# A hybrid attention and convolution block on one core: x loaded a second time in transposed form, and the small vectors as columns

## The chip, the core and the metric

The kernel runs as one program on one core of one Trainium2 chip. The metric is the device time of one execution in microseconds. Before the change it is 1059.32 us, the median of three runs (1058.66 to 1060.2).

Four engines compute: TensorE (PE in the profile, with its weight loads as PEld), VectorE (DVE), ScalarE (ACT) and GpSimd (POOL). SyncE (SP) issues most of the transfers from the chip's memory. Each engine takes its instructions in the order in which the program emits them.

## The reference

One layer over 256 tokens of width 2048, in float32, cut to its course:

```python
xn = rms_norm(x, norm1_g)                      # x: (256, 2048)
q, k, v, ga, gg = split(xn @ w_in)             # 1024 columns each
att = diff_attention(rope(rms_norm(q)), rope(rms_norm(k)), v, lam)
u = ga * sigmoid(gg)
u = silu(layer_norm(causal_depthwise_conv(u, conv_w, conv_b)))   # 31 taps
h = x + concatenate([rms_norm(att), u]) @ w_out
hn = rms_norm(h, norm2_g)
out = h + (silu(hn @ w_gate) * (hn @ w_up)) @ w_down             # hidden 5632
```

## The kernel before

**Products.** A float32 product is made of three matmuls in a shorter format: each operand is split into a rounded part (`hi`) and the rest (`lo`), and hi x hi, lo x hi and hi x lo are summed in PSUM. The tokens are two tiles of 128 rows (m = 0, 1); the weights stream in from memory once.

**Chunks.** All weight work is a list of chunks, mostly of 512 KB. For each chunk the SP queue loads `raw` (line 330), ACT rounds it to `whi` (334), DVE takes the rest `wlo` (343), and PE multiplies: a first half with `whi` (373 and 374) and a second half with `wlo` (379). `raw` has four buffers (tag raw), and every third chunk from chunk 7 on takes one of the two larger `wb` buffers instead (1237). `whi` and `wlo` have four buffers each, so rounding chunk n waits until PE has done chunk n - 4. Up to chunk 4 the rounding is emitted one chunk ahead of the multiplication, from chunk 5 on two chunks ahead (line 476).

The blocks at the start, in the order of the list: the five blocks for the convolution's columns, of which block 0 (chunks 0 to 4, width 256) and block 1 (chunks 5 to 8, width 256) come first; block 2 begins with chunk 9 (width 512). Each block accumulates in two PSUM tiles of the pool `acc`, which has four. Block 2 therefore takes the two tiles that block 0 had.

**Side work.** Everything beside the weight chunks is written as Python generators. Each chunk's `multiply` calls `resume()` twice, after its first half and after its second half (391 and 396), and each call carries every generator to its next `yield`. So a `yield` puts off an emission by half a chunk; the order within each engine's queue is fixed by it. These matter here:

- `x_part` and `x_rest` (498 to 521): x arrives by rows, in five column parts (`XPARTS`, line 54: tiles k = 0-1, 2-3, 4-7, 8-11, 12-15 of 128 columns), into `h`, which also keeps x for the residual. PE transposes each 128 x 128 piece (502), ACT makes `lhi` times the norm's gain (240) and DVE makes `llo` (241). In between, ACT sums the squares of x (491), four column groups of 512 for both m; DVE adds the four sums (518), POOL makes the root `rstd1` (217 and 218), and `normed` is set.
- `glu_done` (535 to 564), one per convolution block: it waits for `normed`, then ACT makes `sig` from the block's sums (544), two resumes later DVE makes `u` from them (549), which is the last use of the block's two PSUM tiles; three resumes later PE transposes `u` (557), and then the 30 taps per channel tile are queued for DVE (569), to be given out by credit: 1.30 a resume, less what other DVE work is charged.
- `gain_columns` (153): the 58 rows of gains and biases are loaded as rows by the ACT queue (148), transposed on PE (155) and copied to `cols` (156).
- `late_constants` (177): the convolution's weights as two tiles of 31 rows (172), the q and k gains and lambda vectors (174), the rotary tables (175), all loaded on the SP queue ahead of chunk 5's weights; PE transposes the convolution's weights in eight pieces (182) and ACT copies them to `cw` (183).
- `warm_up` (140): 14 transposes of the identity at the start, and 5 more after the first part of x.

**The load order on SP** is set by `before` (1252 to 1255): part i of x, two transfers each, stands just ahead of chunk i's weights for i = 0 to 4, and the late constants ahead of chunk 5's.

Of the kernel before, what the change touches and what calls it, by code (L numbers as in the profile page):

```python
# [13 lines left out]
F32 = mybir.dt.float32  # L14
# [5 lines left out]
P = 128  # L20
D = 2048
S = 256
NM = S // P
# [4 lines left out]
CC = 1024  # L28
NCT = CC // P
W = 31  # L30
FF = 5632
KD = D // P
N = 512
# [15 lines left out]

NK = 2  # L50

WARM = (14, 5)

XPARTS = (range(0, 2), range(2, 4), range(4, 8), range(8, 12), range(12, 16))

# [17 lines left out]
HK = KD // 2  # L73
# [35 lines left out]
def tile_block(  # L109
    ctx: ExitStack,  # L110
    tc: tile.TileContext,
    x, conv_w, gains, vecs, rope, wts, out, placed_at,
):
    nc = tc.nc
    PSUM = bass.MemoryType.PSUM
    act, dve, pool, pe, sp = nc.scalar, nc.vector, nc.gpsimd, nc.tensor, nc.sync
# [16 lines left out]
    ident = const.tile([P, P], F32, tag="ident", name="ident")  # L133
# [6 lines left out]
    def warm_up(n):  # L140
        warm = aux_ps.tile([P, N], F32, tag="aux", name="ps_warm")
        for _ in range(n):
            pe.transpose(warm[:, :P], ident, ident)

    warm_up(WARM[0])

    rows = pre.tile([NR, P], F32, tag="rows", name="rows", bufs=1)
    act.dma_start(out=rows, in_=gains)

    act.copy(small.tile([P, 8], F32, tag="rsq", name="first"), neghalf)  # L150
    cols = once.tile([P, NR], F32, tag="cols", name="cols")

    def gain_columns():
        ps = aux_ps.tile([P, N], F32, tag="aux", name="ps_cols")
        pe.transpose(ps[:, :NR], rows, ident[:NR, :NR])
        act.copy(cols, ps[:, :NR])

    def col(key, k):
        return cols[:, AT[key] + k : AT[key] + k + 1]

    cw = pre.tile([P, LINE * 2], F32, tag="cw", name="cw", bufs=1)[:, : NCT * W].rearrange("p (c w) -> p c w", c=NCT)
    gcs = {}
    neg_lam = once.tile([P, 1], F32, tag="neg_lam", name="neg_lam")
    cw_rows = [pre.tile([W, N], F32, tag="va", name="cw_rows") for _ in range(CC // N)]
    rt = pre.tile([P, NM, 2, DH], F32, tag="vb", name="rt")
    gb = pre.tile([P, 2, DH], F32, tag="att", name="gb", bufs=4)
    lamv = pre.tile([P, 4, DH], F32, tag="vc", name="lamv")

    def late_loads():
        flat = conv_w.rearrange("o w i c -> (o w i) c")  # L170
        for i in range(CC // N):
            sp.dma_start(out=cw_rows[i], in_=flat[:, i * N : (i + 1) * N])
        for t, v in ((gb, vecs[:2]), (lamv, vecs[2:])):
            sp.dma_start(out=t, in_=v.rearrange("(o v) d -> o v d", o=1).to_broadcast(list(t.shape)))
        sp.dma_start(out=rt, in_=rope.rearrange("(m p) c d -> p m c d", p=P))

    def late_constants():
        late_loads()
        yield from lag(4)
        pw = aux_ps.tile([P, N], F32, tag="aux", name="ps_cw")  # L180
        for ct in range(NCT):
            pe.transpose(pw[:, ct * W : (ct + 1) * W], cw_rows[ct * P // N][:, ct * P % N : ct * P % N + P], ident[:W, :W])
        act.copy(cw.rearrange("p c w -> p (c w)"), pw[:, : NCT * W])
        while not normed:
            yield
        yield from lag(16)
        act.mul(cols[:, AT["sg"] : AT["sg"] + 2], cols[:, AT["sg"] : AT["sg"] + 2], 1.0 - LAMBDA_INIT)

        act.mul(gb[:, 0, :], gb[:, 0, :], 1.0 / math.sqrt(DH))
        hd = DH // 2  # L190
        for i, key in enumerate("qk"):
            for m in range(NM):
                t = pre.tile([P, 2, DH], F32, tag=f"gcs{key}{m}", name=f"gcs{key}{m}", bufs=1)
                pool.tensor_tensor(t[:, 0, :], rt[:, m, 0, :], gb[:, i, :], ALU.mult)
# [18 lines left out]
    def rsqrt_mean(dst, ss, n, eps):  # L213

        k = dst.shape[-1]
        t = small.tile([P, 8], F32, tag="rsq", name="rsq")
        pool.tensor_scalar(t[:, :k], ss, 1.0 / n, eps, ALU.mult, ALU.add)
        pool.tensor_tensor(dst, t[:, :k], neghalf[:, :k], ALU.pow)
# [5 lines left out]
    def lhs_pair(pfx, k):  # L224
        if k % 2 == 0:
            halves[pfx] = lhs_two(pfx, k)
        return tuple(t[:, k % 2, :] for t in halves[pfx])
# [9 lines left out]
    def split_scaled(pair, src, scale):  # L237

        hi, lo = pair
        act.activation(hi, src, AF.Copy, scale=scale)  # L240
        dve.scalar_tensor_tensor(lo, src, scale, hi.bitcast(F32), ALU.mult, ALU.subtract)  # L241
# [6 lines left out]
    def start(gen):  # L248
        running.append(gen)
# [6 lines left out]
    def lag(n):  # L256
        for _ in range(n):
            yield
# [33 lines left out]
    before = {}  # L292
# [192 lines left out]
    xT = {}  # L485
    rstd1 = [once.tile([P, 1], F32, tag=f"rstd1_{m}", name=f"rstd1_{m}") for m in range(NM)]
    ss1 = [small.tile([P, D // N], F32, tag=f"ss1_{m}", name=f"ss1_{m}", bufs=1) for m in range(NM)]

    def square_sum(src, accum, **kw):
        junk = pre.tile([P, N], F32, tag="junk", name="junk", bufs=1)  # L490
        act.activation(junk[:, : src.shape[-1]], src, AF.Square, accum_out=accum, **kw)

    def x_load(ks):
        cs = slice(ks[0] * P, (ks[-1] + 1) * P)
        for m in range(NM):
            sp.dma_start(out=h[m][:, cs], in_=x[m * P : (m + 1) * P, cs])

    def x_part(ks):
        for k in ks:
            ps = aux_ps.tile([P, N], F32, tag="aux", name="ps_x")  # L500
            for m in range(NM):
                pe.transpose(ps[:, m * P : (m + 1) * P], h[m][:, k * P : (k + 1) * P], ident)
            xT[k] = lhs_pair("x", k)
            split_scaled(xT[k], ps[:, :S], col("g1", k))

    def x_rest():
        c = 0
        for part in XPARTS[1:]:
            x_part(part)
            yield  # L510
            yield
            if part[-1] % (N // P) == N // P - 1:
                for m in range(NM):
                    square_sum(h[m][:, c * N : (c + 1) * N], ss1[m][:, c : c + 1])
                c += 1
        for m in range(NM):
            ss = small.tile([P, 1], F32, tag="ss1", name="ss1")
            dve.tensor_reduce(ss, ss1[m], AX.X, ALU.add)
            rsqrt_mean(rstd1[m], ss, D, EPS)
        yield  # L520
        normed.append(True)
# [728 lines left out]
        j0 += nb  # L1250

    for c, part in enumerate(XPARTS):
        before[c] = lambda part=part: x_load(part)
    before[0] = lambda: (x_load(XPARTS[0]), gain_columns(), x_part(XPARTS[0]), warm_up(WARM[1]), start(x_rest()))
    before[len(XPARTS)] = lambda: start(late_constants())
    run_chunks()


_FLAT = {"x": (S, D), "conv_w": (1, W, 1, CC)}
_WEIGHTS = {"w_in": (D, 5120), "w_out": (D, D), "w_gate": (D, FF), "w_up": (D, FF), "w_down": (FF, D)}  # L1260


# [28 lines left out]
```

## Time and profile before

| what | value |
|---|---|
| median of three runs | 1059.32 us (1058.66 to 1060.2) |
| the profiled execution's own time | 1059.67 us |
| its span in the profile | 1057.9 us |
| mean granted TensorE clock | 0.998 |
| busy share of PE, DVE, ACT, POOL | 98%, 84%, 63%, 13% |
| moved by DMA | 248.10 MB |

The span is the time from the first to the last instruction in the trace; 1.77 us of the profiled execution lie outside it. A timeline row gives the start, the time taken, the engine, the source line, the operation, the written and read tiles, the count of merged instructions, and in brackets the idle time before it with what ended it. A row of the table by stretches gives, for each engine, the busy time and the number of instructions, then the granted clock, the share in which the DMA engines were busy, and the rate.

### The profile page before, as it was taken

Reading aid. Unit: us, or ns where it says so; the run is one execution under the profiler, and the core shown is the slowest. Engines: PE = TensorE matmul, PEld = TensorE weight load, DVE = VectorE, ACT = ScalarE, POOL = GpSimd, SP = SyncE. Lnnn points to the kernel's source line nnn. Section 1 sums busy time; section 2 is a strip of 40 time slices with the busy share of each in tenths; the row PEclk is TensorE's granted clock in tenths of the full one; section 3 lists DMA queues with packets and bytes.
Section 4 is the critical chain, followed back from the end, with each engine's and each line's share of the span. In section 5 each row is a group of like instructions: output and inputs, shape, how many; then the busy total and the mean of one; then the engine's idle time right before and its main releaser. Section 6 shows DMA issues by size and latency. Waiting matters only on the chain.

```text
span 1057.9 us, 13283 instructions
## 1 busy us (share of the span) xinstructions
PE 1038.6 (98%) x4780; PEld 859.5 (81%) x4780; DVE 883.5 (84%) x1103; ACT 667.0 (63%) x852; POOL 136.5 (13%) x182
## 2 busy tenths in 40 slices
PE   8999999999999999999999999999999999999998
PEld 7988888878888887787888888888888888888776
DVE  4799989889666489989979679899896698989984
ACT  6544556757666556676676565776865566668661
POOL 0030023211100100010001120000101111001021
PEclk9999999999999999999999999999999999999999
DMA  8655555454546668997969998979978999879985
GB/s 297 211 176 191 192 178 183 145 171 148 171 140 228 211 209 256 289 265 223 321 198 292 277 308 266 276 225 312 264 228 256 292 289 334 241 223 283 285 216 111
DMA packets 63166, 248.10 MB, mean 235 GB/s; under 512 B 7044, under 2 KB 8510, under 8 KB 55676
## 3 DMA queue, kind: packets, MB, share of 16 engines
q1 hardware_dynamic: 48432, 199.51, 53.3%
q0 software_dynamic: 14608, 47.72, 23.4%
q8 instruction: 37, 0.61, 0.2%
q14 instruction: 29, 0.24, 0.1%
q10 hardware_dynamic: 60, 0.03, 0.0%
HBM read 238.84 MB, written 8.39 MB: 234 GB/s over the span
## 4 chain that ended last, share of the span: by engine, by line
PE 56%; DVE 7%; issue 2%; ACT 1%; POOL 0%; DVEq 0%; ACTq 0%; POOLq 0%
PE q L1074 10%; PE q L1075 10%; PE q L1079 10%; PE q L1053 8%; PE q L1054 8%; PE q L1055 8%; DVE wl L1036 1%; DVE wlo L343 1%; DVE wl L1035 1%; DVE wt L1024 1%; PE ps_a L891 1%; PE acc L379 1%; PE acc L374 1%; PE acc L373 1%; DVE wt L1025 0%
## 5 line engine op out<-in xcount | busy, mean ns | idle before, releaser
L334 ACT CAST whi<-raw 128x1024 fp32r<-128x1024 f32 (+1 forms) x261 | 268.9, 1046 | 116.1 <-PE q L1075 48.5
L343 DVE TENSOR_TENSOR wlo<-raw,whi 128x1024 fp32r<-128x1024 f32 (+1 forms) x188 | 228.0, 1220 | 84.8 <-ACT whi L334 84.6
L373 PE MATMUL acc<-whi,lhi 128*128 128x512 f32 (+1 forms) x448 | 168.6, 381 | 3.4 <-ACT lhi L240 2.7
L374 PE MATMUL acc<-whi,llo 128*128 128x512 f32 (+1 forms) x448 | 167.0, 377 | 0.5 <-DVE llo L241 0.4
L1031 ACT CAST wh<-wt 128x2048 fp32r<-128x2048 f32 x58 | 110.8, 1910 | 38.2 <-DVE wt L1026 37.9
L1036 DVE TENSOR_TENSOR wl<-wt,wh 128x2048 fp32r<-128x2048 f32 x58 | 132.8, 2289 | 2.0 <-ACT wh L1031 1.2
L338 POOL DMA_DIRECT2D wlo<-in_wts_dram x73 | 63.9, 875 | 522.1 <-ACT wlo L337 487.6
L1035 DVE TENSOR_TENSOR wl<-wb,wh 128x1536 fp32r<-128x1536 f32 x58 | 101.7, 1754 | 29.7 <-ACT wh L1030 29.7
L1074 PE MATMUL q<-whi,chi 128*128 128x512 f32 x320 | 125.3, 392 | 0.0
L1075 PE MATMUL q<-whi,clo 128*128 128x512 f32 x320 | 124.6, 389 | 0.0
L379 PE MATMUL acc<-wlo,lhi 128*128 128x512 f32 (+1 forms) x448 | 114.3, 379 | 1.4 <-DVE wlo L343 1.4
L1053 PE MATMUL q<-wh,fhi 128*128 128x512 f32 x280 | 109.8, 392 | 3.1 <-DVE sum L1155 1.4
L1055 PE MATMUL q<-wl,fhi 128*128 128x512 f32 x280 | 109.0, 389 | 0.0
L1054 PE MATMUL q<-wh,flo 128*128 128x512 f32 x280 | 109.0, 389 | 0.0
L569 DVE SCALAR_TENSOR_TENSOR y<-upad,cw,y 128x256 f32<-128x256 f32 x240 | 104.1, 488 | 4.4 <-ACT y L562 3.9
L373 PEld LDWEIGHTS acc<-whi,lhi 128*128 128x128 f32 x448 | 85.3, 190 | 18.9 <-ACT lhi L240 3.1
L374 PEld LDWEIGHTS acc<-whi,llo 128*128 128x128 f32 x448 | 85.5, 191 | 15.7 <-DVE llo L241 0.9
L1030 ACT CAST wh<-wb 128x1536 fp32r<-128x1536 f32 x58 | 85.4, 1473 | 17.5 <-issue 10.9
L379 PEld LDWEIGHTS acc<-wlo,lhi 128*128 128x128 f32 x448 | 79.6, 188 | 16.6 <-DVE wlo L343 2.3
L1079 PE MATMUL q<-wlo,chi 128*128 128x512 f32 x320 | 86.3, 391 | 0.0
L337 ACT ACTIVATE wlo<-raw 128x1024 fp32r<-128x1024 f32 x73 | 77.1, 1056 | 0.0
L1024 DVE TENSOR_TENSOR wt<-wb 128x1024 f32<-128x1024 f32 x58 | 70.8, 1222 | 0.5
(216 smaller groups left out, 1689.1 us busy)
## 6 DMA issues: line engine op xcount, KB each, us to landing
raw<-in_wts_dram SPq DMA_DIRECT2D x259, 512.0 KB, 5.4
wb<-in_wts_dram SPq DMA_DIRECT2D x57, 1024.0 KB, 7.4
wlo<-in_wts_dram POOLq DMA_DIRECT2D x73, 512.0 KB, 8.9
out_dram<-sum POOLq DMA_DIRECT2D x22, 256.0 KB, 6.4
out_dram<-h POOLq DMA_DIRECT2D x8, 256.0 KB, 5.7
h<-in_x_dram SPq DMA_DIRECT2D x6, 256.0 KB, 7.5
wb<-in_wts_dram POOLq DMA_DIRECT2D x1, 1024.0 KB, 8.3
h<-in_x_dram SPq DMA_DIRECT2D x4, 128.0 KB, 3.3
```

Source lines behind the costliest of these rows:

```text
L334: act.copy(c["hi"], c["raw"])
L343: dve.tensor_tensor(c["lo"], c["raw"], c["hi"].bitcast(F32), ALU.subtract)
L373: pe.matmul(ps[m], xhi[:, ms], hi[:, j, :], start=c["first"] and j == 0, stop=False)
L374: pe.matmul(ps[m], xlo[:, ms], hi[:, j, :], start=False, stop=False)
L379: pe.matmul(ps[m], xhi[:, ms], lo[:, j, :], start=False, stop=c["last"] and j == nk - 1)
L1036: dve.tensor_tensor(c["lo"][:, :4], c["t"], c["hi"][:, :4].bitcast(F32), ALU.subtract)
L1053: pe.matmul(ps, fhi[:, f, p, :], c["hi"][:, w], start=bool(first), stop=False)
L1054: pe.matmul(ps, flo[:, f, p, :], c["hi"][:, w], start=False, stop=False)
L1055: pe.matmul(ps, fhi[:, f, p, :], c["lo"][:, w], start=False, stop=bool(last))
L1074: pe.matmul(ps, plain[i][0][:, ms], hi[:, i, :], start=i == 0 and bool(c["first"].get(qs[m])), stop=False)
L1075: pe.matmul(ps, plain[i][1][:, ms], hi[:, i, :], start=False, stop=False)
L1079: pe.matmul(sum_bank(c, qs[m]), plain[i][0][:, ms], lo[:, i, :], start=False, stop=i == 1 and bool(c["last"].get(qs[m])))
```

## The change

The host passes x a second time, transposed: `xt` has 128 rows, and row p holds, for each of the 16 column tiles k, the 256 tokens of column 128 k + p. The gains come transposed as (128, 58), the convolution's weights as (128, 8 x 31).

- The two `wb` buffers hold the transposed x from the start (`halves_of_x`, k = 0-7 and 8-15). Part 0 is loaded by the ACT queue, ahead of the gains, which land directly in `cols`; parts 1 to 4 by the SP queue, one transfer each, ahead of chunks 1 to 4. `lhi` and `llo` are made from these buffers. The PE transposes of x, of the gains and of the convolution's weights are gone, with the copies of the last two, and so are the five later warm-up transposes.
- x by rows is loaded in four transfers of 128 x 1024 (`h_load`), ahead of the weights of chunks 5, 6, 7 and 8. The late constants move behind them, ahead of chunk 9's weights; the convolution's weights are one transfer straight into `cw`.
- `x_rest` makes all parts of x first; the squares come after, two column groups when the loads of that half have been emitted.

```diff
-WARM = (14, 5)
+WARM = 14
...
-    warm_up(WARM[0])
-
-    rows = pre.tile([NR, P], F32, tag="rows", name="rows", bufs=1)
-    act.dma_start(out=rows, in_=gains)
+    warm_up(WARM)
+
+    cols = once.tile([P, NR], F32, tag="cols", name="cols")
+    halves_of_x = [early.tile([P, HK, S], F32, tag="wb", name="xt") for _ in range(2)]
+
+    def x_load(ks, queue):
+        i, k = divmod(ks[0], HK)
+        n = len(ks)
+        queue.dma_start(out=halves_of_x[i][:, k : k + n].rearrange("p k s -> p (k s)"),
+                        in_=xt[:, ks[0] * S : (ks[0] + n) * S])
+
+    x_load(XPARTS[0], act)
+    act.dma_start(out=cols, in_=gains)
...
-    def gain_columns():
-        ps = aux_ps.tile([P, N], F32, tag="aux", name="ps_cols")
-        pe.transpose(ps[:, :NR], rows, ident[:NR, :NR])
-        act.copy(cols, ps[:, :NR])
...
     def late_loads():
-        flat = conv_w.rearrange("o w i c -> (o w i) c")
-        for i in range(CC // N):
-            sp.dma_start(out=cw_rows[i], in_=flat[:, i * N : (i + 1) * N])
+        sp.dma_start(out=cw.rearrange("p c w -> p (c w)"), in_=conv_w)
...
     def late_constants():
         late_loads()
-        yield from lag(4)
-        pw = aux_ps.tile([P, N], F32, tag="aux", name="ps_cw")
-        for ct in range(NCT):
-            pe.transpose(pw[:, ct * W : (ct + 1) * W], cw_rows[ct * P // N][:, ct * P % N : ct * P % N + P], ident[:W, :W])
-        act.copy(cw.rearrange("p c w -> p (c w)"), pw[:, : NCT * W])
         while not normed:
             yield
...
-    def x_load(ks):
-        cs = slice(ks[0] * P, (ks[-1] + 1) * P)
-        for m in range(NM):
-            sp.dma_start(out=h[m][:, cs], in_=x[m * P : (m + 1) * P, cs])
+    def h_load(i):
+        m, cs = i % NM, slice(i // NM * D // 2, (i // NM + 1) * D // 2)
+        sp.dma_start(out=h[m][:, cs], in_=x[m * P : (m + 1) * P, cs])
+        h_loaded.append(i)
+
+    h_loaded = []

     def x_part(ks):
         for k in ks:
-            ps = aux_ps.tile([P, N], F32, tag="aux", name="ps_x")
-            for m in range(NM):
-                pe.transpose(ps[:, m * P : (m + 1) * P], h[m][:, k * P : (k + 1) * P], ident)
             xT[k] = lhs_pair("x", k)
-            split_scaled(xT[k], ps[:, :S], col("g1", k))
+            split_scaled(xT[k], halves_of_x[k // HK][:, k % HK], col("g1", k))

     def x_rest():
-        c = 0
         for part in XPARTS[1:]:
             x_part(part)
             yield
             yield
-            if part[-1] % (N // P) == N // P - 1:
-                for m in range(NM):
-                    square_sum(h[m][:, c * N : (c + 1) * N], ss1[m][:, c : c + 1])
-                c += 1
+        for c in range(D // N):
+            while len(h_loaded) <= c // 2 * NM + 1:
+                yield
+            for m in range(NM):
+                square_sum(h[m][:, c * N : (c + 1) * N], ss1[m][:, c : c + 1])
+            yield
         for m in range(NM):
             ss = small.tile([P, 1], F32, tag="ss1", name="ss1")
             dve.tensor_reduce(ss, ss1[m], AX.X, ALU.add)
             rsqrt_mean(rstd1[m], ss, D, EPS)
         yield
         normed.append(True)
...
-        before[c] = lambda part=part: x_load(part)
-    before[0] = lambda: (x_load(XPARTS[0]), gain_columns(), x_part(XPARTS[0]), warm_up(WARM[1]), start(x_rest()))
-    before[len(XPARTS)] = lambda: start(late_constants())
+        before[c] = lambda part=part: x_load(part, sp)
+    before[0] = lambda: (x_part(XPARTS[0]), start(x_rest()))
+    for i in range(2 * NM):
+        before[len(XPARTS) + i] = lambda i=i: h_load(i)
+    before[len(XPARTS) + 2 * NM] = lambda: start(late_constants())
...
+    given["xt"] = given["x"].reshape(S, KD, P).transpose(2, 1, 0).reshape(P, KD * S)
+    given["conv_w"] = np.asarray(inputs["conv_w"]).reshape(W, NCT, P).transpose(2, 1, 0).reshape(P, NCT * W)
+    given["gains"] = np.concatenate([np.asarray(inputs[name]).reshape(n, P) for name, _, n in ROWS]).T
```

More of the change, by code (lines that the diff above doesn't have):

```diff
@@ L111, in tile_block @@
     tc: tile.TileContext,
-    x, conv_w, gains, vecs, rope, wts, out, placed_at,
+    x, xt, conv_w, gains, vecs, rope, wts, out, placed_at,
 ):
@@ L143, in warm_up @@
             pe.transpose(warm[:, :P], ident, ident)
-    warm_up(WARM[0])
-    rows = pre.tile([NR, P], F32, tag="rows", name="rows", bufs=1)
-    act.dma_start(out=rows, in_=gains)
-    act.copy(small.tile([P, 8], F32, tag="rsq", name="first"), neghalf)
-    cols = once.tile([P, NR], F32, tag="cols", name="cols")
-    def gain_columns():
-        ps = aux_ps.tile([P, N], F32, tag="aux", name="ps_cols")
-        pe.transpose(ps[:, :NR], rows, ident[:NR, :NR])
-        act.copy(cols, ps[:, :NR])
+    warm_up(WARM)
[8 more added lines that the diff above has]
+    act.dma_start(out=cols, in_=gains)
+    act.copy(small.tile([P, 8], F32, tag="rsq", name="first"), neghalf)
     def col(key, k):
@@ L163, in tile_block @@
     neg_lam = once.tile([P, 1], F32, tag="neg_lam", name="neg_lam")
-    cw_rows = [pre.tile([W, N], F32, tag="va", name="cw_rows") for _ in range(CC // N)]
     rt = pre.tile([P, NM, 2, DH], F32, tag="vb", name="rt")
@@ L1252, in tile_block @@
     for c, part in enumerate(XPARTS):
-        before[c] = lambda part=part: x_load(part)
-    before[0] = lambda: (x_load(XPARTS[0]), gain_columns(), x_part(XPARTS[0]), warm_up(WARM[1]), start(x_rest()))
-    before[len(XPARTS)] = lambda: start(late_constants())
+        before[c] = lambda part=part: x_load(part, sp)
[3 more added lines that the diff above has]
+    before[len(XPARTS) + 2 * NM] = lambda: start(late_constants())
     run_chunks()
-_FLAT = {"x": (S, D), "conv_w": (1, W, 1, CC)}
+_FLAT = {"x": (S, D)}
 _WEIGHTS = {"w_in": (D, 5120), "w_out": (D, D), "w_gate": (D, FF), "w_up": (D, FF), "w_down": (FF, D)}
@@ L1269 @@
     given = {name: np.asarray(inputs[name]).reshape(shape) for name, shape in _FLAT.items()}
-    given["gains"] = np.concatenate([np.asarray(inputs[name]).reshape(n, P) for name, _, n in ROWS])
+    given["xt"] = given["x"].reshape(S, KD, P).transpose(2, 1, 0).reshape(P, KD * S)
+    given["conv_w"] = np.asarray(inputs["conv_w"]).reshape(W, NCT, P).transpose(2, 1, 0).reshape(P, NCT * W)
+    given["gains"] = np.concatenate([np.asarray(inputs[name]).reshape(n, P) for name, _, n in ROWS]).T
     given["vecs"] = np.concatenate([np.asarray(inputs[name]).reshape(1, DH) for name in VECS])
```

## The prediction

> **What bounds the kernel now.** I read the page first, its span, its busy times and the chain that ended last, then the timelines of the first 45 us by engine, because every edit lies there.
>
> ```profile
> span 1057.9 us, 13283 instructions
> ...
> PE 1038.6 (98%) x4780; PEld 859.5 (81%) x4780; DVE 883.5 (84%) x1103; ACT 667.0 (63%) x852; POOL 136.5 (13%) x182
> ...
> PE 56%; DVE 7%; issue 2%; ACT 1%; POOL 0%; DVEq 0%; ACTq 0%; POOLq 0%
> ```
>
> PE is busy for 98% of the span: what comes before PE's dense stretch counts one to one, and what runs beside it counts nothing. The question is when PE gets dense, and whether it stays so. PE's timeline:
>
> ```profile
> 14.74 0.38 PE L373 MATMUL acc<-whi,lhi 128*128 128x256 f32 x1 [1.97 <-ACT lhi L240]
> ...
> 18.59 1.03 PE L502 MATMUL ps_x<-ident,h 128*128 128x128 f32 x8
> 19.38 1.20 PE L379 MATMUL acc<-wlo,lhi 128*128 128x256 f32 x8
> ...
> 27.04 0.28 PE L373 MATMUL acc<-whi,lhi 128*128 128x256 f32 x1
> ...
> 29.92 0.28 PE L373 MATMUL acc<-whi,lhi 128*128 128x256 f32 x1
> ...
> 31.93 0.68 PE L182 MATMUL ps_cw<-ident,cw_rows 31*128 31x31 f32 x8
> 32.53 1.21 PE L379 MATMUL acc<-wlo,lhi 128*128 128x256 f32 x8
> ...
> 36.46 0.28 PE L373 MATMUL acc<-whi,lhi 128*128 128x256 f32 x1
> ...
> 38.39 0.38 PE L557 MATMUL ps_u<-ident,u 128*128 128x128 f32 x2
> ...
> 39.56 0.40 PE L373 MATMUL acc<-whi,lhi 128*128 128x512 f32 x1
> ```
>
> Chunk 2 begins at 14.74 after a wait for ACT, chunk 5 at 27.04, chunk 9 (block 2's first) at 39.56. A chunk alone takes 2.88 us (27.04 to 29.92). After 14.74 PE never idles long again, so **39.56 is the mark**: the end moves with the start of chunk 9.
>
> **What the change takes off.** Chunk 2 waited for ACT, whose timeline shows why:
>
> ```profile
> 6.09 0.62 ACT L334 CAST whi<-raw 128x512 fp32r<-128x512 f32 x1
> ...
> 11.90 1.05 ACT L334 CAST whi<-raw 128x1024 fp32r<-128x1024 f32 x1 [2.00 <-DMA raw<-in_wts_dram]
> 12.86 0.63 ACT L491 ACTIVATE junk<-h 128x512 f32<-128x512 f32 x1
> ...
> 14.24 1.55 ACT L240 ACTIVATE lhi<-ps_x,cols 128x256 fp32r<-128x256 f32 x4
> ```
>
> and DVE's timeline has the costs of a chunk there:
>
> ```profile
> 14.72 1.66 DVE L241 SCALAR_TENSOR_TENSOR llo<-ps_x,cols,lhi 128x256 fp32r<-128x256 f32 x4 [0.52 <-ACT lhi L240]
> ...
> 25.31 1.23 DVE L343 TENSOR_TENSOR wlo<-raw,whi 128x1024 fp32r<-128x1024 f32 x1 [0.37 <-ACT whi L334]
> 26.45 0.39 DVE L518 TENSOR_REDUCE ss<-ss 128x1 f32<-128x4 f32 x2
> ```
>
> Two squares stand between `whi` and `lhi`: 14.24 - 12.86 = 1.38 us, gone from there. On PE the transposes of x cost 19.38 - 18.59 = 0.79 in each of chunks 2 and 3, the convolution's weights 32.53 - 31.93 = 0.60. The 5 warm-ups and earlier transposes lie before 14.74, under loads. So chunk 2 could start at 14.74 - 1.38 = 13.36. DVE then needs `wlo` (26.45 - 25.31 = 1.14) and four `llo` (1.66) a chunk, 2.8 us, under PE's 2.88; its late first `llo` costs about 0.8 once (`wlo` stands ahead). Chunk 5 could start at 13.36 + 3 x 2.88 + 0.8 = 22.8, chunk 9 at 22.8 + 4 x 2.88 = 34.3: **5.2 us on offer**, part of which is a slow clock that the trace shows in chunk 2:
>
> ```profile
> 12.78:14.74 1.96, 0.00 (x0) 0.00 (x0) 1.24 (x2) 1.93 (x7) 0.00 (x0) 1.00 1.06 417
> 14.74:18.40 3.66, 3.52 (x15) 3.33 (x16) 2.87 (x5) 3.32 (x8) 0.00 (x0) 0.55 1.01 346
> ```
>
> PE does nothing for 1.96 us, then runs at a granted 0.55. Chunk 2's first half takes 18.59 - 14.74 = 3.85 us against two thirds of 2.88 = 1.92; some 0.3 of it is a wait for `llo`, so one drop costs about 1.6.
>
> **What it adds: a wait ahead of chunk 9.** Chunk 9 writes the two PSUM tiles of block 0, and their last reader is `u` (549), which needs `sig`, which needs `rstd1`, which needs all squares. Before, this was done early:
>
> ```profile
> 32.59 0.60 DVE L549 SCALAR_TENSOR_TENSOR u<-acc,rstd,sig 128x128 f32<-128x128 f32 x2
> ```
>
> `u` was over at 33.2, 6.4 us before 39.56. Now I count the half chunks through the generators. `x_rest` reaches the squares in chunk 4 and finds one `h` load of the two that it needs; chunk 5 emits the loads ahead of chunks 6 and 7, so column groups 0 and 1 are squared in its two halves, groups 2 and 3 in chunk 6's. The sums come in chunk 7's first half, `normed` in its second, `sig` in chunk 8's first, `u` in chunk 9's first, **after** chunk 9's first matmuls and after chunk 11's `whi` and `wlo`. (The same count for the old code puts `u` between the `wlo` of chunks 8 and 9, where DVE's timeline has it.) Nothing locks up, since no one in that chain needs chunk 9; but PE, and all matmuls behind, wait.
>
> ACT's order becomes: `whi` 6, `whi` 7, four squares, `whi` 8, four squares, `whi` 9, `whi` 10, table and `sig`, `whi` 11. It starts when chunk 7's weights land. Before them stand, from chunk 2's weights on: x part 3, weights 3, x part 4, weights 4, then `h`, weights 5, `h`, weights 6, `h`, weights 7: ten transfers of 0.524 MB and 0.03 MB of gains, 5.27 MB. Rates:
>
> ```profile
> 8.00:10.00 2.00, 1.27 (x9) 0.87 (x7) 0.81 (x2) 1.36 (x3) 0.00 (x0) 1.00 0.94 339
> 10.00:12.00 2.00, 1.67 (x14) 1.67 (x15) 0.67 (x2) 0.10 (x1) 0.00 (x0) 1.00 1.01 391
> 12.00:14.00 2.00, 0.78 (x7) 0.57 (x5) 1.02 (x1) 1.97 (x4) 0.00 (x0) 1.00 1.04 409
> 14.00:16.00 2.00, 1.12 (x4) 0.93 (x5) 1.48 (x5) 2.00 (x7) 0.00 (x0) 0.78 1.04 411
> 16.00:18.00 2.00, 2.00 (x12) 2.00 (x11) 1.61 (x2) 1.97 (x5) 0.00 (x0) 0.50 0.99 321
> 18.00:20.00 2.00, 2.00 (x17) 2.00 (x17) 0.49 (x2) 1.09 (x4) 0.00 (x0) 0.87 1.05 332
> ```
>
> With the DMA engines full they moved 409 and 411 GB/s with PE mostly idle; 321 and 332 came when PE was busy and the late constants with their 1 KB rows were among the loads. I take 410 (the nearest, long rows): 5.27 / 0.41 = 12.9 us after chunk 2's 11.90, so chunk 7's weights land at **24.8**. The ends: at 326, 28.1; with the 1.46 MB of 8 to 12 us at 410 too, 0.4 earlier. [...]
>
> From there by rows:
>
> ```profile
> 25.16 0.65 ACT L491 ACTIVATE junk<-h 128x512 f32<-128x512 f32 x1
> ...
> 26.56 1.98 ACT L334 CAST whi<-raw 128x1024 fp32r<-128x1024 f32 x2
> 28.57 1.28 ACT L544 ACT_TABLE_LOAD   x1
> 29.86 0.62 ACT L544 ACTIVATE sig<-acc,rstd 128x128 f32<-128x128 f32 x2
> ...
> 26.96 0.57 POOL L218 TENSOR_TENSOR rstd<-rsq,neghalf 128x1 f32<-128x1 f32 x1
> ...
> 27.89 1.40 POOL L218 TENSOR_TENSOR rstd<-rsq,neghalf 128x1 f32<-128x1 f32 x1
> ```
>
> `whi` 7 takes 0.95 (two in 1.98, the end overlapping); four squares 2 x 1.40 (25.16 to 26.56 is one pair); `whi` 8 0.95; four squares 2.80; `whi` 9 1.05: 8.55. DVE's `wlo` 9 1.14: 9.7. From the sums' start to the second root 29.29 - 26.45 = 2.84: 12.5; the table load lies under it. One `sig` 0.3, `whi` 11 1.05, `wlo` 11 1.14, the first `u` 0.3: **15.3 us**. If the second root takes the 0.57 of a free POOL, 14.5. The late constants are not on it: `whi` 9 begins at 24.8 + 7.5 = 32.3, and weights 9 come two more 0.524 MB, 0.77 MB of constants and 0.524 MB after weights 7, at 410 by 30.5.
>
> Chunk 9 thus starts at 24.8 + 15.3 = 40.1 instead of 34.3, against 39.56 before: **+0.55**. The transposes of block 0's `u`, 0.2 us (chunk 8 took 39.56 - 36.46 = 3.1), now fall behind chunk 9: **+0.2**. PE idles for 5.8 us, so the clock drops as it did after 1.96: **+1.6**, between 0.8 and 2.5 by where the half-speed stretch lies. Sum **+2.4 us**.
>
> **What I cost at nothing.** `lhi` and `llo` read x from the loaded buffers instead of PSUM; no row has that form. ACT's `whi` from such a buffer takes 0.62 for twice the width, `lhi` 0.39 (1.55 for four), so up to 0.23 more each, 0.9 a part, or as much less; ACT waits for weights 7 anyway, that covers it. Part 0 on the ACT queue with gains in rows of 232 bytes: harmless unless it lands after 9.0 (11.90 less 2.8 for four `lhi` and two `whi`); the cover is the same. Weights 7 and 10 now wait on SP for x's buffers: freed when `llo` 7 (about 16) and `llo` 15 (about 21) are done; weights 7 need not move before 24.8 - 0.524 / 0.41 = 23.5, weights 10 later still, so 7 us of earlier loads cover it; without them each us late would add one. The convolution: taps start 2.5 chunks later, but by counting the credits through the code the last is emitted half a chunk later (chunk 86's first half instead of 85's second). Its slack:
>
> ```profile
> 291.48 0.29 DVE L634 CAST mchi<-z 128x256 fp32r<-128x256 f32 x1 [0.69 <-ACT z L631]
> ...
> 294.26 0.48 PE L373 MATMUL acc<-whi,mchi 128*128 128x512 f32 x1
> ```
>
> 2.78 us against half a chunk, 1.4; a whole chunk more would cost some 1.5.
>
> **The rivals.** (a) *The loads are no faster than 326 GB/s once PE is dense*: landing at 28.1, +3.3, so +5.7 in all: 1065.4. For it: 321 and 332; against it: the small rows in them. (b) *The same wait, but shorter*: loads 0.4 earlier, the root at 0.57, the clock drop at 0.8: 2.4 - 0.4 - 0.8 - 0.8 = +0.4, 1060.1. (c) *The other side: no wait before chunk 9*, because `rstd1` is there earlier than I count, or the tiles are not shared as I read; it decides once `u` is over by 34.3, some 6 us sooner than my 40.1. Then -5.2 + 0.2 = -5.0: 1054.7; with a slow stretch in chunks 0 to 4, 1056.3. [...] The trace shows a drop after 1.96. For (c) speaks only that the old `u` had 6.4 us to spare; against it, the order of emission. (d) *The change doesn't do what it says*, PE's early loads being bound by bytes: chunk 2 then stays at 14.74, which the wait at chunk 9 hides; the time is the forecast's.
>
> **How the numbers follow.** The sum is made against the profiled execution, 1059.67, which is 0.35 above the median of 1059.32: 1062.07, less 0.35 gives 1061.7; the rivals as given stand on 1059.67. I take **1061.8**. A measurement of this kernel can tell about 0.2% (2.1 us) from no change, so slower begins at 1061.4 and faster ends at 1057.2. Chances: forecast (with d) 0.50, from 1060.2 to 1064 (three fifths of it slower); (a) 0.16, slower; (b) 0.20, within; (c) 0.14, faster, and 0.02 more from the tail of (b). So slower 0.46, within 0.2% 0.38, faster 0.16. Cases of both signs hold it; the forecast's own range is 1060.2 to 1064. Leaving out most of (c) and the end of (a): 1056.5 to 1065.5.
>
> **What would show it.** PE: chunk 5 near 22.8, a gap of 4 to 6 us ending near 40 with the release by DVE's line 549, then a granted clock near 0.5. ACT: eight squares between about 25.7 and 32.3, `sig` near 37. Wrong if PE has no gap ahead of chunk 9, if weights 7 land far from 24.8, or if a gap opens near 294 before line 373's `mchi`.

## The result, and the profile after

The changed kernel takes 1060.87 us (median of 13 runs, 1060.04 to 1062.85), the kernel before 1059.01 us (13 runs): ratio 1.0021, 95% interval 1.0013 to 1.003. It is slower by about two microseconds. The profiled execution took 1062.85 us, the longest of the 13, so its trace shows more loss (3.2 us of span) than the median has (1.9 us). The page after, its head, its busy times and PE's costliest group (busy time and mean ns, then the idle time before it):

```profile
span 1061.1 us, 13189 instructions
...
PE 1036.1 (98%) x4734; PEld 856.6 (81%) x4734; DVE 882.1 (83%) x1103; ACT 667.4 (63%) x850; POOL 138.1 (13%) x182
...
L368 PE MATMUL acc<-whi,lhi 128*128 128x512 f32 (+1 forms) x448 | 169.5, 383 | 9.6 <-DVE u L544 6.9
```

PE lost 46 matmuls and 2.5 us of busy time, and the span still grew. The last number says where to look: of the 9.6 us in which this group let PE idle, 6.9 end with DVE's `u`. (The lines of the changed kernel: 368, 369 and 374 are the matmuls, 329 `whi`, 338 `wlo`, 486 the squares, 539 `sig`, 544 `u`, 629 `mchi`.) PE's timeline after:

```profile
7.33 0.58 PE L368 MATMUL acc<-whi,lhi 128*128 128x256 f32 x1 [2.73 <-ACT whi L329]
...
7.92 0.42 PE L368 MATMUL acc<-whi,lhi 128*128 128x256 f32 x1
8.14 0.41 PE L369 MATMUL acc<-whi,llo 128*128 128x256 f32 x1
...
11.81 0.28 PE L368 MATMUL acc<-whi,lhi 128*128 128x256 f32 x1
...
20.55 0.28 PE L368 MATMUL acc<-whi,lhi 128*128 128x256 f32 x1
...
31.11 1.12 PE L374 MATMUL acc<-wlo,lhi 128*128 128x256 f32 x8
39.10 0.77 PE L368 MATMUL acc<-whi,lhi 128*128 128x512 f32 x1 [6.87 <-DVE u L544]
...
47.37 0.38 PE L552 MATMUL ps_u<-ident,u 128*128 128x128 f32 x2
47.51 0.48 PE L368 MATMUL acc<-whi,lhi 128*128 128x512 f32 x1
...
49.45 1.08 PE L374 MATMUL acc<-wlo,lhi 128*128 128x512 f32 x4
...
297.53 0.50 PE L368 MATMUL acc<-whi,mchi 128*128 128x512 f32 x1 [0.57 <-DVE mchi L629]
...
298.33 0.40 PE L368 MATMUL acc<-whi,mchi 128*128 128x512 f32 x1
```

Chunk 2 begins at 11.81 and chunk 5 at 20.55, where the kernel before had 14.74 and 27.04: at chunk 5 PE is 6.5 us ahead. Then it is done with chunk 8 at 39.10 - 6.87 = 32.23 and stands still for 6.87 us. Chunk 9 starts 0.46 us ahead of the old 39.56, and the lead of 6.5 is spent. What holds it is read from ACT, DVE and POOL after:

```profile
9.18 1.04 ACT L329 CAST whi<-raw 128x1024 fp32r<-128x1024 f32 x1 [0.57 <-DMA raw<-in_wts_dram]
...
23.27 1.05 ACT L329 CAST whi<-raw 128x1024 fp32r<-128x1024 f32 x1 [2.75 <-DMA raw<-in_wts_dram]
24.22 0.63 ACT L486 ACTIVATE junk<-h 128x512 f32<-128x512 f32 x1
...
27.11 1.03 ACT L329 CAST whi<-raw 128x1024 fp32r<-128x1024 f32 x1
...
30.94 1.98 ACT L329 CAST whi<-raw 128x1024 fp32r<-128x1024 f32 x2
...
36.13 0.37 ACT L539 ACTIVATE sig<-acc,rstd 128x128 f32<-128x128 f32 x1 [0.54 <-POOL rstd L213]
36.40 1.03 ACT L329 CAST whi<-raw 128x1024 fp32r<-128x1024 f32 x1
```

```profile
33.14 0.21 DVE L513 TENSOR_REDUCE ss<-ss 128x1 f32<-128x4 f32 x2
33.27 1.22 DVE L338 TENSOR_TENSOR wlo<-raw,whi 128x1024 fp32r<-128x1024 f32 x1
37.47 1.23 DVE L338 TENSOR_TENSOR wlo<-raw,whi 128x1024 fp32r<-128x1024 f32 x1 [2.98 <-ACT whi L329]
38.61 0.60 DVE L544 SCALAR_TENSOR_TENSOR u<-acc,rstd,sig 128x128 f32<-128x128 f32 x2
```

```profile
33.39 1.15 POOL L212 TENSOR_SCALAR rsq<-ss 128x1 f32<-128x1 f32 x1 [31.77 <-DVE ss L513]
34.62 0.57 POOL L213 TENSOR_TENSOR rstd<-rsq,neghalf 128x1 f32<-128x1 f32 x1
35.27 0.19 POOL L212 TENSOR_SCALAR rsq<-ss 128x1 f32<-128x1 f32 x1
35.55 0.55 POOL L213 TENSOR_TENSOR rstd<-rsq,neghalf 128x1 f32<-128x1 f32 x1
```

The reader sees the counted order of emission: chunk 7's `whi` as its weights land (23.27), four squares, chunk 8's `whi`, four squares, two `whi`, the sums (33.14), the roots, `sig`, chunk 11's `whi` and `wlo`, and only then `u`. The stretches of the profile (length, then PE, PEld, DVE, ACT and POOL with busy time and count, then granted clock, DMA share, GB/s), four of after and one of before:

```profile
4.00:9.18 5.18, 2.45 (x11) 2.05 (x10) 2.76 (x6) 2.75 (x7) 0.00 (x0) 1.00 1.02 392
9.18:23.27 14.09, 14.09 (x113) 14.04 (x112) 10.82 (x18) 9.83 (x18) 0.00 (x0) 1.00 1.02 408
...
34.66:39.10 4.44, 0.00 (x1) 0.03 (x1) 1.64 (x3) 1.70 (x4) 1.27 (x3) 0.50 0.67 216
39.10:44.90 5.80, 5.80 (x14) 4.56 (x15) 1.86 (x4) 1.53 (x3) 0.00 (x0) 0.50 0.53 184
```

```profile
4.00:11.90 7.90, 6.10 (x43) 5.02 (x42) 3.04 (x6) 2.91 (x7) 0.00 (x0) 1.00 0.94 298
```

The early loads ran at 392 GB/s instead of 298, and at 408 while PE was busy without a break. After the gap the clock is 0.50 until 44.90. Where the 3.2 us of the profiled run went: chunk 9's start, -0.46; the slow clock, 2.7 (worked out below); the transposes of `u`, 47.51 - 47.37 = 0.14; and a wait that was not there before, for `mchi` at 297.53, 0.57 and some 0.26 in the rows behind it (298.33 - 297.53 = 0.80 to the next `mchi` product, 0.54 before). The sum is +3.2, but it closes a little better than it should. By positions, PE is 2.70 behind the kernel before when it is free for `mchi` (296.96 against 294.26), where the first three terms give 2.4, and 3.53 behind at the next `mchi` product (298.33 against 294.80). So some 0.3 us ahead of that wait is in none of the terms, and as much is won back behind it; neither was followed up.

### The profile page after: what moved, and what is told of

Read it like the earlier page. It is cut to its first block, busy times and chain, and to the rows that moved or that the text cites. A ratio compares the mean times of both kernels' runs of the same rounds, so it can differ in the third digit from the quotient of the medians.

```text
span 1061.1 us, 13189 instructions
## 1 busy us (share of the span) xinstructions
PE 1036.1 (98%) x4734; PEld 856.6 (81%) x4734; DVE 882.1 (83%) x1103; ACT 667.4 (63%) x850; POOL 138.1 (13%) x182
## 4 chain that ended last, share of the span: by engine, by line
PE 55%; DVE 6%; issue 2%; ACT 1%; DMA 0%; POOL 0%; DVEq 0%; ACTq 0%; POOLq 0%
PE q L1069 10%; PE q L1070 10%; PE q L1074 10%; PE q L1048 8%; PE q L1049 7%; PE q L1050 7%; DVE wl L1031 1%; DVE wl L1030 1%; DVE wt L1019 1%; PE ps_a L886 1%; DVE wlo L338 1%; PE acc L374 1%; PE acc L369 1%; PE acc L368 1%; DVE wt L1020 0%
```

## The experiments

**Theory 1**: chunk 9 waits for the PSUM tiles that `u` frees; `u` is late because the squares begin when chunk 7's weights land. **Rivals**: the loads set chunk 9 whatever the tiles do; the cost is the clock after the gap, not the gap's end; the loss lies in the other edits.

### Other tiles for block 2

Chunk 9 takes its two accumulators from the auxiliary PSUM pool (`spare`), and gives them back once `u` has read them (`held`); `c0 == 2` is block 2.

```diff
+        if c0 == 2:
+            held[0] -= NM
...
-              lambda ps, c0=c0, nct=nct: glu_done(c0, nct, ps), cuts=[len(p) for p in XPARTS] if c0 == 0 else ())
+              lambda ps, c0=c0, nct=nct: glu_done(c0, nct, ps), cuts=[len(p) for p in XPARTS] if c0 == 0 else (),
+              spare=c0 == 2)
```

> Block 2 accumulates in two tiles of the auxiliary PSUM pool, so chunk 9 no longer needs block 0's tiles; loads, order of ACT and DVE and everything else as in the changed kernel. Theory 1 (chunk 9 waits for the last read of block 0's tiles, and that wait with its clock drop is all that the change loses): chunk 9 starts where chunk 8 ends, near 32 us instead of 39.1, no clock drop after it, so 7.0 plus 1.5 to 2.9 us less than the changed kernel's 1060.9: about 1052, between 1051 and 1054. A new wait of up to 1 us at chunk 11 is possible, whose whi follows sig on ACT (37.4 in the changed kernel, chunk 11 due at 37.4). Theory 2 (the 2.1 MB of x by rows ahead of chunks 5 to 8 hold back the weights, and the wait only covers it): chunk 9 stays near 39, 1060.9.

Measured: 1053.55 us (1052.55 to 1054.08), ratio to the kernel before 0.9948 (0.9936 to 0.996). PE's timeline of this run:

```profile
32.91 0.40 PE L368 MATMUL acc<-whi,lhi 128*128 128x512 f32 x1
...
288.91 0.49 PE L368 MATMUL acc<-whi,mchi 128*128 128x512 f32 x1 [0.57 <-DVE mchi L631]
```

Chunk 9 starts 6.65 us before the old 39.56, without a wait. Less 0.2 for `u`'s transposes and 0.8 at `mchi`, that is -5.65, and the medians differ by 5.65 (1059.2 in that comparison; the runs spread over 1.5 us, so so close an agreement is chance). With everything else as in the changed kernel, the borrowed tiles give 7.3 us back: theory 1 holds.

### The norm of x left out

```diff
-        for c in range(D // N):
-            while len(h_loaded) <= c // 2 * NM + 1:
-                yield
-            for m in range(NM):
-                square_sum(h[m][:, c * N : (c + 1) * N], ss1[m][:, c : c + 1])
-            yield
-        for m in range(NM):
-            ss = small.tile([P, 1], F32, tag="ss1", name="ss1")
-            dve.tensor_reduce(ss, ss1[m], AX.X, ALU.add)
-            rsqrt_mean(rstd1[m], ss, D, EPS)
+        for m in range(NM):
+            pool.memset(rstd1[m], 1.0)
```

> The norm of x is left out: its factor is set to 1 and no squares are taken, while x by rows is loaded at the same places. Theory 1: u of block 0 is read in chunk 6, chunk 9 starts near 32, about 1052 as for the kernel with the spare PSUM tiles; the 5.5 us of squares that ACT no longer has are worth nothing more. Theory 2: the loads are the same, so chunk 9 stays near 39 and the time at 1060.9.

Measured: 1051.93 us (1051.31 to 1052.56), ratio 0.9934 (0.9921 to 0.9947). PE's timeline of this run:

```profile
32.97 0.40 PE L368 MATMUL acc<-whi,lhi 128*128 128x512 f32 x1
```

Chunk 9 starts at 32.97, without a wait and with all loads in place, so the loads do not set it; the chain through the squares does. The wait for `mchi` is gone too, as the taps can start earlier there; that fits a wait that comes from the same lateness of the norm.

### The gap filled with transposes of the identity

```diff
+FILL = 60
...
+        if c is chunks[9]:
+            warm_up(FILL)
```

> 60 transposes of the identity ahead of chunk 9's first matmul, 0.107 us each, 6.4 us, in the gap of 6.9 us. The wait stays and chunk 9 starts at 39.1. If the clock drop behind the gap costs what I took (0.8 to 2.5 us) and transposes hold the clock: granted clock 1.0 through 40 to 45, and 1.0 to 2.9 us less than 1060.9, about 1059.3. If transposes do not hold it: 0.5 as before, 1060.9. If the clock is only a record without a price: 1.0 and 1060.9.

Measured: 1059.92 us (1058.89 to 1060.65), ratio 1.0007 (0.9998 to 1.0015). Its PE timeline, and the stretch of the gap in the form given above:

```profile
32.84 6.71 PE L144 MATMUL ps_warm<-ident 128*128 128x128 f32 x60
39.31 0.48 PE L371 MATMUL acc<-whi,lhi 128*128 128x512 f32 x1
...
46.93 1.07 PE L377 MATMUL acc<-wlo,lhi 128*128 128x512 f32 x4
```

```profile
32.84:39.31 6.47, 6.47 (x62) 6.47 (x61) 2.29 (x4) 3.28 (x7) 1.91 (x4) 1.00 0.70 235
```

Chunk 9 starts 0.2 us later than in the changed kernel, but at a granted clock of 1.00 (39.00 to 45.00) instead of 0.50, and chunk 11 reaches its `wlo` products at 46.93 instead of 49.45: the drop cost 2.5 + 0.2 = 2.7 us in the changed kernel's profiled run. Over many runs the two kernels differ by about 1.5 us by the ratios (1.0021 against 1.0007 of 1059) and by 1.1 by the medians, each against its own runs of the kernel before. The two intervals overlap a little, so this is a rough size, and rather too small: in this profiled run `u` began at 37.51, 1.10 ahead of the changed kernel's 38.61, but the transposes were still running and held chunk 9 until 39.31. With the clock held, the loss of 1.9 us comes down to 0.7, which is not told apart from none. So the clock makes up most of the measured loss, and the wait of 6.9 us itself takes the gain away.

### x by rows loaded ahead of chunk 5's weights

```diff
-    for i in range(2 * NM):
-        before[len(XPARTS) + i] = lambda i=i: h_load(i)
+    before[len(XPARTS)] = lambda: [h_load(i) for i in range(2 * NM)]
```

> All four loads of x by rows stand ahead of chunk 5's weights, so that the squares are emitted from chunk 4 on and u in chunk 8, ahead of chunk 9's first matmul. Bytes up to chunk 8's weights are the same. Theory 1: chunk 5 starts 1 to 1.5 us later (its weights land 3.8 us later and had over 2 to spare), u is done near 37.5, chunk 9 starts 1.6 us sooner than 39.1, the clock drop stays or is shorter: 1.6 to 2.5 us less than 1060.9, about 1059. Theory 2: weights 5 to 7 come later, so it is 2 to 4 us slower: 1063 to 1065.

Measured: 1059.75 us (1057.57 to 1061.5), ratio 1.0007 (0.9998 to 1.0015). In the profiled run, PE's timeline and the stretch of its gap:

```profile
37.58 0.47 PE L368 MATMUL acc<-whi,lhi 128*128 128x512 f32 x1 [2.97 <-DVE u L544]
```

```profile
34.60:37.58 2.98, 0.01 (x2) 0.04 (x1) 1.64 (x3) 2.24 (x3) 0.00 (x0) 1.00 0.51 173
```

Chunk 9 came where it was expected, 1.5 us sooner, and the time fell by about as much; but the weights behind those loads land later (PE waits for `whi` 3.9 us in all instead of 2.7), and PE still stands for 2.97: no cure. The clock held through this gap of 2.97 us and behind it (granted 1.00 from 34.60 to 44.00), whereas a gap of 1.96 us in the kernel before was followed by a drop (granted 0.55 from 14.74 to 18.40). This execution was the fastest of the twelve; ten of them have a mean clock of 0.996 to 0.998, so the clock did drop in most.

### Only the gains and the convolution's weights as columns

```diff
-    rows = pre.tile([NR, P], F32, tag="rows", name="rows", bufs=1)
-    act.dma_start(out=rows, in_=gains)
+    cols = once.tile([P, NR], F32, tag="cols", name="cols")
+    act.dma_start(out=cols, in_=gains)
...
-        flat = conv_w.rearrange("o w i c -> (o w i) c")
-        for i in range(CC // N):
-            sp.dma_start(out=cw_rows[i], in_=flat[:, i * N : (i + 1) * N])
+        sp.dma_start(out=cw.rearrange("p c w -> p (c w)"), in_=conv_w)
```

(on the kernel before; the PE transposes of both and their copies go as well)

> The kernel before with one part of the change alone: gains and convolution weights come as columns, x as before by rows with its transposes. Every theory: the eight transposes of the convolution's weights go from chunk 6 (0.60 us on PE), those of the gains lie ahead of the loads and are worth nothing: 0.6 us less than before, about 1058.6. If it is more than 1.5 us away from before, this part has an effect that I missed.

Measured: 1057.11 us (1055.94 to 1058.93) against 1058.45, ratio 0.9989 (0.9981 to 0.9998). PE's timeline of this run:

```profile
38.95 0.40 PE L358 MATMUL acc<-whi,lhi 128*128 128x512 f32 x1
```

Chunk 9 is 0.61 us sooner than 39.56. Ahead of the eight transposes PE was 0.17 behind the kernel before (the `wlo` products of chunk 4 start at 26.25 and 26.08), so they are worth 0.78 rather than the expected 0.60. The medians differ by 1.34, because more of its runs had no drop of the clock at all: among runs with a mean clock of 1.000 the medians are 1056.36 (7 runs) and 1057.16 (5), among those at 0.998 1057.87 (4) and 1058.57 (8): 0.7 to 0.8 either way. Why more of its runs had no drop was not looked into. This part of the change is a gain.

### Other tiles, and the taps on a smaller charge

```diff
-TAP_US = 0.396
+TAP_US = 0.39
```

(on the kernel with other tiles for block 2)

> The kernel with the spare PSUM tiles, and the charge of a tap set from 0.396 to 0.39, by which the last tap is emitted half a chunk earlier, where the kernel before had it (second half of chunk 85). Theory: the later taps cost the wait of PE for mchi, 0.57 us, and about 0.3 in that chunk; with the old place both go: 0.9 us less than 1053.55, about 1052.6, and no wait of line 368 for mchi. Rival: the wait comes from something else (aux tiles held by block 2): it stays, 1053.5.

Measured: 1052.19 us (1051.38 to 1056.1), ratio 0.9944 (0.9931 to 0.9958). PE's timeline:

```profile
290.39 0.48 PE L368 MATMUL acc<-whi,mchi 128*128 128x512 f32 x1
```

No wait stands behind that row any more: a smaller charge lets the last tap out in time. The time against the run with other tiles alone (0.9948) is not told apart. Of the versions that compute everything its median is the lowest, some 0.56% under the kernel before. In the profiled execution, the slowest of the five at 1056.1, chunk 7's weights landed 1.0 us later than with other tiles alone (`whi` 7 at 23.95 against 22.95), and PE then waited 1.21 us for `u` ahead of its transposes at 39.69. So with the other tiles the chain is out of chunk 9's way, but has little room left.

### One load more, ahead of chunk 7's weights, then behind them

```diff
         h_loaded.append(i)
+        if i == 2:
+            sp.dma_start(out=v_sb[0], in_=x[:P, : H * E])
```

(with `i == 3` in the second kernel)

> The changed kernel with one more load of 0.524 MB (x again, into a buffer that is written later) ahead of chunk 7's weights. If ACT's chain starts with the landing of weights 7, as predicted: whi 7 at 24.5 instead of 23.3, chunk 9 at 40.4 instead of 39.1. If the chain starts with chunk 6's weights or with the first squares' loads: chunk 9 at 39.1.

> The same load one step later, ahead of chunk 8's weights. If the chain starts with weights 7: whi 7 at 23.3, and chunk 9 between 39.1 and 39.5 (weights 9 may land a little behind whi 9's turn at 30.9). If it starts with weights 8 or 9: chunk 9 at 40.4.

Measured, one run each: 1064.33 and 1064.42 us. The first fence is from ACT's and PE's timelines with the load ahead of chunk 7's weights, the second with the load behind them:

```profile
24.61 1.05 ACT L329 CAST whi<-raw 128x1024 fp32r<-128x1024 f32 x1 [3.53 <-DMA raw<-in_wts_dram]
...
40.45 0.77 PE L368 MATMUL acc<-whi,lhi 128*128 128x512 f32 x1 [7.69 <-DVE u L546]
```

```profile
22.62 1.05 ACT L329 CAST whi<-raw 128x1024 fp32r<-128x1024 f32 x1 [1.50 <-DMA raw<-in_wts_dram]
...
38.78 0.77 PE L368 MATMUL acc<-whi,lhi 128*128 128x512 f32 x1 [5.95 <-DVE u L546]
```

The rows of ACT are `whi` 7. Ahead of chunk 7's weights the load moves `whi` 7 and chunk 9 by 1.34 and 1.35 us, 15.84 between them, as in the changed kernel (39.10 - 23.27 = 15.83). Behind them the interval is 16.16; the start lies below the expected 39.1 to 39.5, because in that run chunk 7's weights landed 0.65 earlier. So it is the landing of chunk 7's weights that starts the chain, and a load behind them adds only 0.3. The second run's total is as high although chunk 9 began earlier; its trace shows a second drop of the clock, to a granted 0.50 from 406.5 to 409.9, behind a gap of 1.74 us on PE.

### Why the early loads were faster: three ways to cut them

The rate of 392 GB/s had not been foreseen. Rows of 2 and 4 KB instead of 1 and 2 KB are the first guess. Each load of the transposed x was cut in two: by rows, by halves of the partitions, by even and odd partitions.

```diff
-        queue.dma_start(out=halves_of_x[i][:, k : k + n].rearrange("p k s -> p (k s)"),
-                        in_=xt[:, ks[0] * S : (ks[0] + n) * S])
+        for j in (0, n // 2):
+            queue.dma_start(out=halves_of_x[i][:, k + j : k + j + n // 2].rearrange("p k s -> p (k s)"),
+                            in_=xt[:, (ks[0] + j) * S : (ks[0] + j + n // 2) * S])
```

```diff
+        for p in (0, P // 2):
+            queue.dma_start(out=halves_of_x[i][p : p + P // 2, k : k + n].rearrange("p k s -> p (k s)"),
+                            in_=xt[p : p + P // 2, ks[0] * S : (ks[0] + n) * S])
```

```diff
+        for p in range(2):
+            queue.dma_start(out=halves_of_x[i][p::2, k : k + n].rearrange("p k s -> p (k s)"),
+                            in_=xt[p::2, ks[0] * S : (ks[0] + n) * S])
```

> The changed kernel with each load of the transposed x cut in two along its rows: twice the transfers, rows of 1 KB (parts 0 and 1) and 2 KB (parts 2 to 4), the row lengths of the kernel before, instead of 2 and 4 KB. The bytes, the order and the rest stay. Theory 'rows': the early loads were faster after the change (392 GB/s from 4.00 to 9.18, when chunk 2's whi begins, against 298 from 4.00 to 11.90 before) because of the longer rows. Then the rate falls to about 300, the 2.03 MB take 6.8 us instead of 5.2, whi 2 begins near 10.8, whi 7 near 24.5 to 25 and chunk 9 near 40.5, with a total of some 1.5 us above the 1062.85 of the changed kernel's profiled run (or as much above its median). Theory 'order': the loads are faster for another reason (fewer small constants among them, x no longer in the way of the weights); then whi 2 stays within 0.4 us of 9.18, whi 7 within 0.7 of 23.27, chunk 9 within 0.7 of 39.10.

> The control to the run with half rows: each load of the transposed x is cut in two as well, but by partitions (64 and 64), so that there are as many transfers and as many issues on the queues of ACT and SP, with the long rows of 2 and 4 KB. Theory 'rows': the early rate stays at 380 to 400 GB/s, whi 2 begins within 0.4 us of 9.18, chunk 9 within 0.7 of 39.10. If it is the number of transfers or their issue (0.4 us each on SP) that costs, this run is as late as the one with half rows.

> A second control to the run with half rows, in place of the one with halves of 64 partitions, whose loads went at 176 to 283 GB/s up to 20 us: each load of the transposed x is cut in two by even and odd partitions, so both halves spread over the whole width; as many transfers and issues as with half rows, but rows of 2 and 4 KB. If the length of the rows makes the difference, whi 2 begins within 0.4 us of 9.18 (with half rows: 10.05), whi 7 within 0.5 of 23.27 (24.41) and chunk 9 within 0.5 of 39.10 (40.25). If the number of transfers or their issue does, the three lie at the values of the half rows. In either case chunk 9 begins 15.8 us after whi 7.

Measured, one run each: 1063.55, 1067.58 and 1063.76 us. The same stretch of the three, in that order:

```profile
4.00:10.00 6.00, 3.37 (x20) 2.97 (x19) 2.97 (x6) 2.75 (x6) 0.00 (x0) 0.86 0.98 300
```

```profile
4.00:10.00 6.00, 0.43 (x3) 0.19 (x1) 0.83 (x2) 1.53 (x5) 0.00 (x0) 0.79 1.08 210
```

```profile
4.00:10.00 6.00, 2.33 (x11) 1.93 (x10) 2.63 (x6) 2.89 (x7) 0.00 (x0) 1.00 0.86 298
```

Over the same six microseconds the kernel before moved 268 GB/s and the changed one 397. Half rows bring it down to 300; so does the cut by even and odd partitions, which keeps the long rows. `whi` 2 began at 10.05 with half rows and at 10.51 with alternate partitions, against 9.18. So **the theory of the rows is not shown**: with the long rows kept, twice the transfers are as slow. It is not excluded either. The DMA share differs: with half rows the DMA engines are busy for 0.98 of the stretch, with alternate partitions for 0.86, so the two may be slow for different reasons, short rows among them. Whether it is the issue on SP, the order of landing or the transfers themselves stays open, and with it why the early loads got faster. The halves of 64 partitions are slower still, with the DMA engines full (last section), and say nothing on the number of transfers. Chunk 9 began at 40.25, 45.69 and 40.91, and `whi` 7 at 24.41, 29.85 and 25.08: 15.84, 15.84 and 15.83 us earlier, an interval that five runs (with the changed kernel and the load ahead of chunk 7's weights) agree on.

## Why the prediction came out as it did, step by step

- **The mark (39.56, PE dense behind it)** held: -6.65 at chunk 9 gave -5.65 in the time, the difference named above.
- **The offer, 5.2 us** (chunk 9 at 34.3), was too small: 7.3 in the changed kernel (32.23) and 6.65 with other tiles. The step that was off is "chunk 2 could start at 13.36": it took two squares off the old 14.74 but left chunk 2's weights at 11.90, where they landed by 9.18. The 0.8 for a late first `llo` did not show either: chunks 2 to 4 took (20.55 - 11.81) / 3 = 2.91 each. Even 7.3 has a slow stretch in it: the products of chunks 0 and 1 came 0.21 us apart until 10.70 (7.92, 8.14), as in the slow stretch of the kernel before (15.64 to 18.20); from 10.85 on they came 0.12 apart.
- **The added wait** stood where the count had put it, released by `u`, with the order of ACT as listed. The other tiles for block 2 show it as the cause, since the change alone moved no other wait of that size.
- **Chunk 7's weights at 24.8**: 23.27. The rate was right, 410 against 408. The start was 2.7 too late (11.90 for 9.18), and 14.09 us at 408 are 5.75 MB instead of 5.27, 1.2 us too few: together 1.5. Rival (a), 326 GB/s once PE is dense, falls: 408 came with PE busy for all of the 14.09 us. Rival (d) falls with chunk 2 at 11.81.
- **The chain, 15.3 us**: 15.83. Up to the sums 9.87 (said 9.7), the roots 2.96 (33.14 to 36.10; said 2.84), from there to chunk 9 3.0 (said 2.8).
- **`lhi` and `llo` from loaded buffers, at nothing**: four `lhi` took 1.71 us instead of 1.55 and four `llo` 1.67 as before (1.66); ACT's wait of 2.75 ahead of `whi` 7 covers it, as said.
- **Chunk 9 at 40.1**: 39.10, so -0.46 instead of +0.55. The errors in landing (-1.5) and chain (+0.5) partly cancel.
- **The clock, 1.6 (0.8 to 2.5)**: about 1.1 to 1.5 over the runs, or somewhat more, and 2.7, above the stated end, in the profiled one.
- **The taps at nothing** was wrong: 0.8 us. The count of half a chunk (1.4) was set against a slack of 2.78, but the way from the last tap to `mchi` also falls behind two `wlo` on DVE. DVE's timeline of the kernel before, then of the changed kernel (the statistics of the layer norm behind the taps, what gathers them into `mv`, then `mchi`):

```profile
283.01 1.28 DVE L600 BATCH_NORM_STATS2 stats<-upad 128x6 f32<-128x512 f32 x2
284.20 0.32 DVE L609 BATCH_NORM_AGGREGATE mv<-stats 128x2 f32<-128x12 f32 x2
```

```profile
287.05 1.28 DVE L595 BATCH_NORM_STATS2 stats<-upad 128x6 f32<-128x512 f32 x2
288.24 1.21 DVE L338 TENSOR_TENSOR wlo<-raw,whi 128x1024 fp32r<-128x1024 f32 x1
289.37 0.27 DVE L604 BATCH_NORM_AGGREGATE mv<-stats 128x2 f32<-128x12 f32 x2
...
296.05 1.23 DVE L338 TENSOR_TENSOR wlo<-raw,whi 128x1024 fp32r<-128x1024 f32 x1 [5.32 <-ACT whi L329]
297.19 0.29 DVE L629 CAST mchi<-z 128x256 fp32r<-128x256 f32 x1
```

  PE was free at 297.53 - 0.57 = 296.96, so `mchi` began 0.23 after it, not 2.78 ahead: a slip of 3.0. Measured from where PE is free (294.26 and 296.96), the last statistics slip by 1.34, the half chunk; `mv` by 2.47, as a `wlo` now stands between the two; `mchi` by 3.01, with another `wlo` just ahead of it. With the charge of 0.39 the last tap is back in its old place, and the wait is gone.
- **The sum, +2.4**: over the runs -0.46 + 1.5 + 0.14 + 0.8 = +2.0 (+1.6 with 1.1 for the clock), measured +1.86. The mechanism is the forecast's, and the other tiles show it. That the time is so close is in part luck: two of its terms were off in opposite directions, the start by -1.0 and the taps by +0.8.
- **The time, 1061.8 (1060.2 to 1064)**: 1060.87. By the prediction's own line of 0.2% the result, +0.18%, lies within and not among the slower, although 13 runs do tell it from none (1.0013 to 1.003). By the time alone rival (b), a shorter wait, is no farther off (1060.1 against 1060.87; the forecast was 1061.8). What speaks against (b) are its terms: the landing was earlier by 1.5 instead of 0.4, but the second root in 0.55 us did not shorten the roots, since the first `rsq` took 1.15, and the clock cost more than 0.8. (c) is what the other tiles bring about, 1053.55 where it said 1054.7; the profiled run took 1053.69 with a mean clock of 0.998, and for a slow stretch in chunks 0 to 4 it had said 1056.3.

## What to carry to other kernels

Before work is taken off a start-up path, list who shares buffers across it: here two accumulators that had been free 6.4 us ahead of time became the next limit, and a pair of idle PSUM tiles turned a loss of 1.9 us into a gain of 5.7. When a chain moves, find the one event that starts it (here one landing, with 15.84 us behind it) and move that or cut the chain. A slack has to be counted against everything queued on the engine that delivers, not against the slip alone.

## What the hardware showed beside that

- **The clock dropped in stretches whose ends were not those of the gaps.** At a granted clock of 0.50 were 3.41 us before (15.10 to 18.51, where the gap ended at 14.74), 3.40 us with the load behind chunk 7's weights (406.5 to 409.9), and three times as much after (10.24 us, 34.66 to 44.90, where the gap lasted from 32.23 to 39.10). A gap of 1.96 us was followed by a drop and one of 2.97 was not, and the clock cost 1.1 to 1.5 us on average but 2.7 in one run; what sets the start of such a stretch is not shown. Within the kernel before, runs with and without a drop differ by 1058.57 - 1057.16 = 1.4 us.
- **The mean clock of a run did not give what a drop cost.** Of the 13 runs of the changed kernel the nine with a mean clock of 0.995 have a median of 1060.41 us, the four with 0.997 one of 1061.73; in the profiled run 4.44 of the 10.24 us at half clock lay in the gap, where PE had nothing to do. And the granted clock reads 1.00 from 4.00 to 9.18 after, although the products there came 0.21 us apart instead of 0.12: that slow stretch is missing from it.
- **Transposes of the identity held the clock**: with 60 of them in the gap, 6.5 us long, it was granted at 1.00 from 32.84 to 39.31, where the changed kernel had 0.50 from 34.66 on.
- **Loads into 64 partitions brought the rate down to about half**: 210 GB/s from 4.00 to 10.00, with the DMA engines fully busy (1.08), against 397 in the changed kernel (1.03). Weights into 128 partitions were loaded in the same stretch, so 210 is not the rate of a load into 64 partitions alone; why the rate fell is not shown.
- **A tiny operation on POOL took six times as long beside one on DVE**, seen once: `rsq` 1.15 us from 33.39 while DVE made `wlo` (33.27 to 34.49), and 0.19 at 35.27, alone.
